# The inverse of the delta rule two units later, and the norm of its output on VectorE

## The chip, the cores and the metric

The kernel runs on one core of a Trainium2 chip. The metric is the device time of one execution, in microseconds (us); of several executions the median is taken. The core's engines are named as in the profile: PE (TensorE, the matmuls), PEld (its weight loads), DVE (VectorE), ACT (ScalarE), POOL (GpSimd) and SP, which here only issues DMAs. Each engine works through its own instructions in the order of the program, and waits on semaphores for the others.

## What is computed

Two blocks run one after the other on 256 positions of width 1024, all in float32. The first has a gated short convolution, a gated delta rule of 8 heads (its output is y_b), and a feed-forward part with a convolution; the second has dilated attention, retention and a feed-forward part. The change touches the delta rule. Its reference, cut to what matters (T is the 256 positions; the kernel uses two chunks of 128 where the reference has four of 64, which is the same function):

```
proj = rmsnorm(x) @ w_in;  bg, cg, xv, q, k, v, z, a, b, ga, gb = split(proj)
y_a = (bg * conv(cg * xv)) @ w_a_out
# delta rule, for each head and chunk:
L = strict_lower((k*beta) @ k.T) * decay
u, w = solve(I + L, [v*beta, k*beta*exp(G)])     # "the inverse"
o = chunked scan over (q, k, u, w)
o = o * rsqrt(mean(o*o) + EPS) * norm_g          # "the norm of its output"
y_b = (o * silu(z)) @ w_b_out
mix = sigmoid(ga) * y_a + sigmoid(gb) * y_b;  x = x + mix @ w_o
```

## The kernel before, in words

**Dense work in units.** Every weight matrix is cut into jobs of one block of 1 MB (128 partitions by 2048 floats), and nearly every job into two units of half a block. A unit is 24 matmuls of 256 columns (line 355): a weight half is split by ACT into a high part H (line 165) and by DVE into the rest L (line 168), and the three products high x high, high x low and low x high are summed. In the delta rule's neighbourhood the jobs come in this order: v's columns of w_in (4 jobs), w_a_out (4), then the columns of ga, z and gb (4 each), then w_b_out (4). The blocks come into three buffers "raw" by DMAs on SP's queue (line 337); the load of a job is issued when the last split of the job three before it is done. There are three buffers each for H and L, and a unit's split stands in the program two units ahead of its matmuls.

**The delta rule between the units.** The loop over units lets generators advance: after each unit's matmuls every open generator runs to its next `yield`, so a `yield` is the way to move work one unit later. The order of the instructions on every engine follows from where the yields stand. If a unit's input isn't there yet when its matmuls are to be written, `drain` advances the generators until it is, and what they write then stands ahead of the unit.

**The inverse.** `subst` inverts the 32x32 blocks of the triangular matrices by substitution, on DVE and then on POOL (tile ebd, with bt for the products). The result goes through DRAM: POOL writes ebd to a scratch tensor (scr), transposes it and writes it again, and eight DMAs (line 633, four on POOL's queue, four on SP's) bring the blocks to the tiles Em and Dm. `for _ in range(SC_Z): yield` then counts off units, and `sub_ok` lets `gdn_main` go on: line 688 multiplies Dm by U, lines 690, 691, 709 and 711 merge the blocks into the whole inverse, one batch per unit. Then follow the transposes of v (725), the products with the inverse (754), and those of o (766, 771, 743, 744).

**The norm and the way out.** The sums of squares of o are made by ACT (tile jk, into so). POOL scales them, DVE seeds the inverse root fo, POOL makes three Newton steps (helper `rsqrt`), and POOL multiplies o by fo, eight times. Four yields later PE transposes o in four pieces of two heads (line 808), one piece per unit; DVE multiplies a piece by g and zs, ACT writes its high part to Oh, and DVE the rest to Ol. Oh and Ol together are `ob`, the input of w_b_out's units. A unit of w_b_out uses half of the heads: the first half the pieces 0 and 1, the second half the pieces 2 and 3.

Of the kernel before, what the change touches and what calls it, by code (L numbers as in the profile page):

```python
# [8 lines left out]
I32 = mybir.dt.int32  # L9
# [3 lines left out]
MUL, ADD, SUB = ALU.mult, ALU.add, ALU.subtract  # L13

EPS = 1e-6
# [16 lines left out]
SG_Y = {8: 3, 0: 4, 16: 5}  # L32
U_Y = 1
SC_Y = 2
SC_Z = 6
EXP1 = 1


# [60 lines left out]
def _build(tc, nc, A, ACT, DVE, POOL, PE, SP, raw_p, hl_p, c_p, b_p, t_p, m_p, s_p, d_p, x_p):  # L99
    uid = [0]  # L100

    def nm(s):
        uid[0] += 1
        return f"{s}{uid[0]}"
# [33 lines left out]
    def free(*ts):  # L138
        for t in ts:
            tag, long = tag_of.pop(id(t))[0:2]  # L140
            free_tags[long].insert(0, tag)

    def tmp(tag, shape=(2, 256), dt=F32, bufs=None):
        return t_p.tile([128] + list(shape), dt, tag=tag, name=nm(tag), **({"bufs": bufs} if bufs else {}))

    def cst(name, shape, dt=F32):
        return c_p.tile(list(shape), dt, tag=name, name=name)
# [19 lines left out]
    def tt(eng, out, a, b, op):  # L167
        eng.tensor_tensor(out=out, in0=a, in1=b, op=op)  # L168

    def stt(out, in0, scalar, in1, op0, op1):  # L170
        DVE.scalar_tensor_tensor(out=out, in0=in0, scalar=scalar, in1=in1, op0=op0, op1=op1)

    def ts(out, in0, s1, op0, s2=None, op1=None):
        if s2 is None:
            DVE.tensor_scalar(out=out, in0=in0, scalar1=s1, scalar2=None, op0=op0)
        else:
            DVE.tensor_scalar(out=out, in0=in0, scalar1=s1, scalar2=s2, op0=op0, op1=op1)
# [8 lines left out]
    def pts(out, in0, s1, op0, s2=None, op1=None):  # L186
        if s2 is None:
            POOL.tensor_scalar(out=out, in0=in0, scalar1=s1, scalar2=None, op0=op0)
        else:
            POOL.tensor_scalar(out=out, in0=in0, scalar1=s1, scalar2=s2, op0=op0, op1=op1)  # L190

    def rsqrt(y, v, n, steps=3, dve=False):
        a = tmp(f"nw{n}", (n,))
        DVE.tensor_scalar(out=y.bitcast(I32), in0=v.bitcast(I32), scalar1=-0.5, scalar2=float(0x5F3759DF), op0=MUL, op1=ADD)
        for _ in range(steps):
            if dve:
                tt(DVE, a, y, y, MUL)
                stt(a, a, -0.5, v, MUL, MUL)
                stt(y, a, 1.5, y, ADD, MUL)
                continue  # L200
            tt(POOL, a, y, y, MUL)
            tt(POOL, a, a, v, MUL)
            pts(a, a, -0.5, MUL, 1.5, ADD)
            tt(POOL, y, y, a, MUL)
# [245 lines left out]
    def gates():  # L450
# [34 lines left out]
        yield  # L485
        yield from gdn_decay()
        yield from gdn_main()

    def gdn_norm_k():
# [84 lines left out]
    def gdn_main():  # L574
# [3 lines left out]
        srk, bk2, rqs = (gd[k] for k in ("srk", "bk2", "rqs"))  # L578
# [23 lines left out]
        def subst():  # L602
# [31 lines left out]
            free(ebd)  # L634
            for _ in range(SC_Z):
                yield
# [28 lines left out]
        a = tmp("nw16", (16,))  # L665
# [6 lines left out]
        rq2 = cst("ss2", [128, 2, 8]).rearrange("p c h -> p (c h)")  # L672
# [111 lines left out]
        sof = so.rearrange("p c h -> p (c h)")  # L784
        fo = cst("fo", [128, 16])
        yield
        tt(POOL, sof, sof, rq2, MUL)
        POOL.tensor_scalar(out=sof, in0=sof, scalar1=1.0 / 128, scalar2=EPS, op0=MUL, op1=ADD)
        yield
        rsqrt(fo, sof, 16)  # L790
        tt(POOL, fo, fo, rqs, MUL)
        for h2 in range(4):
            for c in range(2):
                sl = slice(8 * c + 2 * h2, 8 * c + 2 * h2 + 2)
# [896 lines left out]
```

## Time and profile before

| | us |
|---|---|
| median of 3 executions (1129.2 to 1130.95) | 1130.07 |
| the profiled execution | 1132.15 |
| its span in the trace | 1130.4 |
| PE busy in the span | 1107.6 |
| DVE busy | 755.6 |
| ACT busy | 584.9 |
| POOL busy | 242.9 |

PE is busy nearly all the time, so what counts is where it stands still and where its clock is low. In the page's forty slices the granted clock (1.0 is full speed, 2.4 GHz; 0.5 is 1.2 GHz) is below 0.9 in one slice alone, the seventh (170 to 198 us), which also has PE's lowest busy share. The views below look there, and then at the end of the delta rule.

### The profile page before, as it was taken

The page shows a single profiled execution, that of the slowest core. Times are in us where ns is not written, and L with a number is a line of the kernel's source. Part 1 is how long each engine was busy: PE and PEld are TensorE (multiplying, and loading weights), DVE is VectorE, ACT ScalarE, POOL GpSimd, SP SyncE. Part 2 cuts the span into 40 slices and gives each one's busy share as a digit, 9 for nine tenths or more (in the row PEclk, how much of TensorE's full clock was granted, in tenths as well). Part 3 has the DMA queues.
Part 4 walks back from the last instruction along what each step waited for, and adds up shares of the span by engine and source line. Part 5 has one row for each costly group of instructions (what it writes and reads, how often), then busy time and mean ns, then how long its engine had stood idle before and what let it go on. Part 6 is the DMA issues. An engine that isn't in the chain of part 4 may idle for free.

```text
span 1130.4 us, 20225 instructions
## 1 busy us (share of the span) xinstructions
PE 1107.6 (98%) x8340; PEld 1051.7 (93%) x8340; DVE 755.6 (67%) x1033; ACT 584.9 (52%) x944; POOL 242.9 (21%) x245
## 2 busy tenths in 40 slices
PE   9999897999999999999999999999999999999998
PEld 8989897999999999999878899889999999999997
DVE  4978995344577988778854567556686658655554
ACT  6866253266555444443687554445475445444442
POOL 2565796010401221222200500001340001000000
PEclk9999998999999999999999999999999999999999
DMA  8456347343555565554575544354447555565662
GB/s 262 128 186 186 118 149 197 102 150 112 187 187 169 169 210 193 193 183 162 185 260 182 186 150 150 126 189 133 150 143 227 189 186 166 180 197 190 194 192 75
DMA packets 155087, 194.82 MB, mean 172 GB/s; under 512 B 5678, under 2 KB 132005, under 8 KB 154740
## 3 DMA queue, kind: packets, MB, share of 16 engines
q1 hardware_dynamic: 153888, 191.57, 52.1%
q0 software_dynamic: 912, 1.43, 0.6%
q8 instruction: 65, 1.06, 0.4%
q10 hardware_dynamic: 196, 0.54, 0.1%
q14 instruction: 26, 0.21, 0.1%
HBM read 191.68 MB, written 1.84 MB: 171 GB/s over the span
## 4 chain that ended last, share of the span: by engine, by line
PE 82%; POOL 4%; DVE 2%; ACT 2%; issue 1%; DMA 1%; DVEq 0%; ACTq 0%; POOLq 0%
PE d L355 61%; PE x L355 13%; POOL ebd L168 2%; POOL bt L168 2%; DVE L L168 1%; ACT H L165 1%; DMA Dm<-scr 1%; ACT jk L165 1%; PE x L688 0%; PE x L1206 0%; PE x L1231 0%; PE x L690 0%; ACT w L165 0%; PE x L1265 0%; PE x L691 0%
## 5 line engine op out<-in xcount | busy, mean ns | idle before, releaser
L168 DVE TENSOR_TENSOR L<-raw,H 128x1024 fp32r<-128x1024 f32 x354 | 445.3, 1264 | 241.2 <-ACT H L165 240.9
L165 ACT ACTIVATE H<-raw 128x1024 fp32r<-128x1024 f32 (+1 forms) x355 | 369.4, 1053 | 188.8 <-PE d L355 122.3
L355 PE MATMUL d<-Hh,L 128*128 128x256 f32 x576 | 79.7, 281 | 8.0 <-DVE L L168 8.0
L355 PE MATMUL d<-nh,H 128*128 128x256 f32 x608 | 84.1, 280 | 0.0
L355 PE MATMUL d<-nl,H 128*128 128x256 f32 x608 | 84.1, 280 | 0.0
L355 PE MATMUL d<-nh,L 128*128 128x256 f32 x608 | 83.7, 279 | 0.0
L355 PE MATMUL d<-Hh,H 128*128 128x256 f32 x576 | 81.6, 284 | 0.7 <-ACT H L165 0.7
L355 PEld LDWEIGHTS d<-Hh,L 128*128 128x128 f32 x576 | 72.1, 188 | 10.1 <-DVE L L168 10.0
L355 PE MATMUL d<-Hl,H 128*128 128x256 f32 x576 | 79.1, 280 | 0.0
L355 PEld LDWEIGHTS d<-nh,H 128*128 128x128 f32 x608 | 77.6, 188 | 1.1
L355 PEld LDWEIGHTS d<-nl,H 128*128 128x128 f32 x608 | 76.8, 188 | 0.0
L355 PEld LDWEIGHTS d<-nh,L 128*128 128x128 f32 x608 | 76.7, 188 | 0.0
L355 PEld LDWEIGHTS d<-Hh,H 128*128 128x128 f32 x576 | 71.7, 188 | 1.1 <-ACT H L165 1.0
L355 PEld LDWEIGHTS d<-Hl,H 128*128 128x128 f32 x576 | 72.5, 188 | 0.0
L355 PE MATMUL d<-H,x2h 128*128 128x512 f32 x208 | 57.4, 398 | 0.8 <-ACT H L165 0.8
L355 PE MATMUL d<-H,x2l 128*128 128x512 f32 x208 | 57.0, 396 | 0.0
L355 PE MATMUL d<-L,x2h 128*128 128x512 f32 x208 | 56.4, 393 | 0.0
L355 PE MATMUL d<-x2h,H 128*128 128x256 f32 x384 | 54.2, 284 | 0.0
L355 PE MATMUL d<-x2l,H 128*128 128x256 f32 x384 | 52.7, 280 | 0.0
L355 PE MATMUL d<-x2h,L 128*128 128x256 f32 x384 | 52.3, 279 | 0.0
L165 ACT ACTIVATE w<-w 128x512 f32<-128x512 f32 (+1 forms) x35 | 21.7, 619 | 53.2 <-POOL w L168 22.0
L355 PEld LDWEIGHTS d<-x2h,H 128*128 128x128 f32 x384 | 48.5, 189 | 0.6
(403 smaller groups left out, 1943.7 us busy)
## 6 DMA issues: line engine op xcount, KB each, us to landing
raw<-in_w_in_dram SPq DMA_DIRECT2D x86, 1024.0 KB, 5.1
raw<-in_w_up_dram SPq DMA_DIRECT2D x38, 1024.0 KB, 5.3
raw<-in_w_down_dram SPq DMA_DIRECT2D x27, 1024.0 KB, 4.9
raw<-in_w_proj_b_dram SPq DMA_DIRECT2D x8, 1024.0 KB, 5.4
raw<-in_w_a_out_dram SPq DMA_DIRECT2D x4, 1024.0 KB, 9.1
raw<-in_w_b_out_dram SPq DMA_DIRECT2D x4, 1024.0 KB, 5.3
raw<-in_w_o_dram SPq DMA_DIRECT2D x4, 1024.0 KB, 5.9
raw<-in_w_out_dram SPq DMA_DIRECT2D x4, 1024.0 KB, 5.4
```

Of the source, the lines that this page charges most:

```text
L165: ACT.activation(out=out, in_=in_, func=func, **kw)
L168: eng.tensor_tensor(out=out, in0=a, in1=b, op=op)
L355: PE.matmul(out, lhsT=x if swap else w, rhs=w if swap else x, start=first and ps == 0, stop=last and ps == group[-1] and group is (order o ...
```

## The change

The constant SC_Z, the number of units between the DMAs into Em and Dm and the rest of the inverse, goes from 6 to 8. The norm of o is made on DVE alone: the scaling of so, the seed, the three Newton steps (three instructions each, where POOL had four) and the product with rqs. The seed and the first step stand behind the first `yield`, the other two steps behind the second. The products of o by fo stay on POOL.

```
-SC_Z = 6
+SC_Z = 8
...
         fo = cst("fo", [128, 16])
         yield
-        tt(POOL, sof, sof, rq2, MUL)
-        POOL.tensor_scalar(out=sof, in0=sof, scalar1=1.0 / 128, scalar2=EPS, op0=MUL, op1=ADD)
-        yield
-        rsqrt(fo, sof, 16)
-        tt(POOL, fo, fo, rqs, MUL)
+        tt(DVE, sof, sof, rq2, MUL)
+        ts(sof, sof, 1.0 / 128, MUL, EPS, ADD)
+        a = tmp("nw16", (16,))
+        DVE.tensor_scalar(out=fo.bitcast(I32), in0=sof.bitcast(I32), scalar1=-0.5, scalar2=float(0x5F3759DF), op0=MUL, op1=ADD)
+        for k in range(3):
+            tt(DVE, a, fo, fo, MUL)
+            stt(a, a, -0.5, sof, MUL, MUL)
+            stt(fo, a, 1.5, fo, ADD, MUL)
+            if k == 0:
+                yield
+        tt(DVE, fo, fo, rqs, MUL)
         for h2 in range(4):
...
```

On PE, where the inverse goes on, the order of before is this (Hh and Hl are the input's high and low part for v's columns; yah and yal are w_a_out's input; each group of three rows is a unit):

```order
L355 MATMUL d_2257<-Hh_114,H_2211 128x256 x8
L355 MATMUL d_2257<-Hl_115,H_2211 128x256 x8
L355 MATMUL d_2257<-Hh_114,L_2212 128x256 x8
L688 MATMUL x_2315<-Dm_1342,U_1114 128x64 x8
L355 MATMUL d_2338<-yah_1242,H_2249 128x256 x8
L355 MATMUL d_2338<-yal_1243,H_2249 128x256 x8
L355 MATMUL d_2338<-yah_1242,L_2250 128x256 x8
L688 MATMUL x_2365<-Dm_1342,U_1114 128x64 x8
L355 MATMUL d_2338<-yah_1242,H_2283 128x256 x8
```

and the order of the changed kernel at the same place is this:

```order
L355 MATMUL d_2257<-Hh_114,H_2211 128x256 x8
L355 MATMUL d_2257<-Hl_115,H_2211 128x256 x8
L355 MATMUL d_2257<-Hh_114,L_2212 128x256 x8
L355 MATMUL d_2329<-yah_1242,H_2249 128x256 x8
L355 MATMUL d_2329<-yal_1243,H_2249 128x256 x8
L355 MATMUL d_2329<-yah_1242,L_2250 128x256 x8
L355 MATMUL d_2329<-yah_1242,H_2283 128x256 x8
L355 MATMUL d_2329<-yal_1243,H_2283 128x256 x8
L355 MATMUL d_2329<-yah_1242,L_2284 128x256 x8
L688 MATMUL x_2387<-Dm_1342,U_1114 128x64 x8
L355 MATMUL d_2402<-yah_1242,H_2321 128x256 x8
```

The two batches of line 688 moved behind the two units of w_a_out's first job.

On PE, at the end of the delta rule, the order of before has a unit behind each of the transposes of o (the last two of the four stand here), and w_b_out's first unit (the one with Oh) after that:

```order
L808 MATMUL x_3589<-cmats,o_2834 128x128 x4
L355 MATMUL d_3599<-Hh_114,H_3517 128x256 x8
L355 MATMUL d_3599<-Hl_115,H_3517 128x256 x8
L355 MATMUL d_3599<-Hh_114,L_3518 128x256 x8
L808 MATMUL x_3628<-cmats,o_2834 128x128 x4
L355 MATMUL d_3599<-Hh_114,H_3555 128x256 x8
L355 MATMUL d_3599<-Hl_115,H_3555 128x256 x8
L355 MATMUL d_3599<-Hh_114,L_3556 128x256 x8
L355 MATMUL d_3672<-Oh_3509,H_3595 128x256 x8
```

and the changed kernel (where line 814 is the old line 808) has this:

```order
L814 MATMUL x_3607<-cmats,o_2896 128x128 x4
L355 MATMUL d_3578<-Hh_114,H_3536 128x256 x8
L355 MATMUL d_3578<-Hl_115,H_3536 128x256 x8
L355 MATMUL d_3578<-Hh_114,L_3537 128x256 x8
L814 MATMUL x_3646<-cmats,o_2896 128x128 x4
L814 MATMUL x_3661<-cmats,o_2896 128x128 x4
L355 MATMUL d_3656<-Oh_3566,H_3574 128x256 x8
L355 MATMUL d_3656<-Ol_3567,H_3574 128x256 x8
L355 MATMUL d_3656<-Oh_3566,L_3575 128x256 x8
L355 MATMUL d_3656<-Oh_3566,H_3613 128x256 x8
```

The dense units between the last transposes and w_b_out are gone, and the fourth transposes stand right behind the third.

On DVE, the pieces 2 and 3 of before (w is the product of a transposed piece, g and zs) stand with a weight's low part between them:

```order
L168 TENSOR_TENSOR L_3596<-raw_3422,H_3595 128x1024
L171 SCALAR_TENSOR_TENSOR w_3624<-x_3589,prm,zs_3132 128x512
L168 TENSOR_TENSOR Ol_3510<-w_3624,Oh_3509 128x512
L168 TENSOR_TENSOR L_3634<-raw_3422,H_3633 128x1024
L171 SCALAR_TENSOR_TENSOR w_3663<-x_3628,prm,zs_3132 128x512
L168 TENSOR_TENSOR Ol_3510<-w_3663,Oh_3509 128x512
```

and in the changed kernel they stand like this:

```order
L168 TENSOR_TENSOR L_3653<-raw_3480,H_3652 128x1024
L171 SCALAR_TENSOR_TENSOR w_3657<-x_3646,prm,zs_3101 128x512
L168 TENSOR_TENSOR Ol_3567<-w_3657,Oh_3566 128x512
L171 SCALAR_TENSOR_TENSOR w_3666<-x_3661,prm,zs_3101 128x512
L168 TENSOR_TENSOR Ol_3567<-w_3666,Oh_3566 128x512
L168 TENSOR_TENSOR L_3695<-raw_3480,H_3694 128x1024
```

The fourth piece now follows the third directly, and the next weight's low part comes behind both.

## Rows read from the trace of the kernel before

**Rows 1.** Page, part 1: engine, busy us (share of the span), instructions.
```profile
PE 1107.6 (98%) x8340; PEld 1051.7 (93%) x8340; DVE 755.6 (67%) x1033; ACT 584.9 (52%) x944; POOL 242.9 (21%) x245
```
**Rows 2.** Who waited for whom, PE, whole run: us in total, times, longest us.
```profile
PE d L355 <- DVE L L168: 8.0, 8, 2.5
PE x L688 <- DMA Dm<-scr: 6.6, 1, 6.6
```
**Rows 3.** Order of time: start, us, engine, line, operation, out<-in, count [idle before <-releaser].
```profile
174.61 1.09 PE L355 MATMUL d<-Hh,L 128*128 128x256 f32 x8
...
176.04 13.38 SPq L337 DMA_DIRECT2D raw<-in_w_a_out_dram  x4
...
182.34 3.65 PE L688 MATMUL x<-Dm,U 128*128 128x64 f32 x16 [6.65 <-DMA Dm<-scr]
184.02 2.00 ACT L165 ACTIVATE H<-raw 128x1024 fp32r<-128x1024 f32 x2 [3.80 <-DMA raw<-in_w_a_out_dram]
...
185.75 2.06 PE L355 MATMUL d<-yah,H 128*128 128x256 f32 x8
...
190.75 1.89 PE L688 MATMUL x<-Dm,U 128*128 128x64 f32 x16
...
192.45 1.19 PE L355 MATMUL d<-yah,H 128*128 128x256 f32 x8
```
**Rows 4.** Who waited for whom, SP's queue, 140 to 235 us.
```profile
SPq L633 <- DMA scr<-ebd: 16.0, 2, 13.9
```
**Rows 5.** Stretches: length, each engine's busy us (instructions), PEclk, DMA share, GB/s.
```profile
180.00:182.30 2.30, 0.00 (x0) 0.00 (x0) 0.00 (x0) 0.22 (x1) 0.52 (x1) 0.53 1.08 328
...
189.00:190.00 1.00, 1.00 (x7) 1.00 (x6) 1.00 (x2) 0.45 (x1) 1.00 (x1) 0.50 0.02 5
190.00:191.00 1.00, 1.00 (x9) 1.00 (x9) 1.00 (x1) 1.00 (x2) 1.00 (x2) 0.80 0.69 179
...
206.80:208.00 1.20, 1.20 (x10) 1.18 (x9) 1.07 (x3) 0.00 (x0) 0.00 (x0) 0.78 1.08 384
208.00:210.00 2.00, 2.00 (x11) 2.00 (x11) 0.00 (x1) 0.00 (x0) 0.00 (x0) 0.50 0.31 108
210.00:211.00 1.00, 1.00 (x7) 1.00 (x7) 0.00 (x0) 0.00 (x0) 0.00 (x0) 0.56 0.00 0
```
**Rows 6.** Order of time again, at the third and fourth transposes of o.
```profile
305.03 0.60 PE L808 MATMUL x<-cmats,o 128*128 128x128 f32 x4
...
305.39 1.17 PE L355 MATMUL d<-Hh,H 128*128 128x256 f32 x8
...
306.07 0.63 ACT L165 ACTIVATE Oh<-w 128x512 fp32r<-128x512 f32 x1 [1.96 <-DVE w L171]
...
306.73 0.69 DVE L168 TENSOR_TENSOR Ol<-w,Oh 128x512 fp32r<-128x512 f32 x1 [0.70 <-ACT Oh L165]
...
308.17 1.23 DVE L168 TENSOR_TENSOR L<-raw,H 128x1024 fp32r<-128x1024 f32 x1 [0.74 <-ACT H L165]
308.26 0.60 PE L808 MATMUL x<-cmats,o 128*128 128x128 f32 x4
...
309.31 0.74 DVE L171 SCALAR_TENSOR_TENSOR w<-x,prm,zs 128x512 f32<-128x512 f32 x1
...
310.09 0.63 ACT L165 ACTIVATE Oh<-w 128x512 fp32r<-128x512 f32 x1 [1.95 <-DVE w L171]
...
310.75 0.69 DVE L168 TENSOR_TENSOR Ol<-w,Oh 128x512 fp32r<-128x512 f32 x1 [0.70 <-ACT Oh L165]
```
**Rows 7.** Groups by line on DVE, 128 to 142 us and 360 to 368: busy us, mean ns.
```profile
L168 DVE TENSOR_TENSOR nw<-grr 128x16 f32<-128x16 f32 x3 | 1.7, 569 | 0.0
...
L168 DVE TENSOR_TENSOR nw<-sr 128x2 f32<-128x2 f32 x3 | 0.5, 161 | 0.1
```
**Rows 8.** Order of time, behind the norm: a low part and PE's use of it.
```profile
288.39 1.22 DVE L168 TENSOR_TENSOR L<-raw,H 128x1024 fp32r<-128x1024 f32 x1
...
292.13 1.09 PE L355 MATMUL d<-Hh,L 128*128 128x256 f32 x8
```

## The prediction

> **What bounds the kernel now.** The page's first part has TensorE (PE) busy for 98% of the span [rows 1]; PE runs the matmuls in the order of the program, so a matmul that waits holds up all behind it. The second view is who waited for whom: the longest single wait of the run is 6.6 us, PE at line 688 (first matmuls of the inverse) for the DMA into Dm; next come eight waits for DVE's low parts, 8.0 us together, 2.5 us the longest [rows 2]. The third view is the instructions in order of time around that wait [rows 3]: PE ends the last unit of V at 175.7, stands until 182.34, runs line 688, and starts the first unit of w_a_out at 185.75.
>
> The reader should now ask what stands behind the removed wait. The block of w_a_out was issued on SP's queue at 176.04, and ACT's split of it into H waited for that DMA until 184.02 [rows 3]. The queue was held up itself: SP waited 16.0 us at line 633 for the scratch results of the substitution, 13.9 us at a stretch [rows 4]. So two transfers end late here, the blocks of Dm at 182.34 and the weights at 184.02, and only the first shows as a wait of PE, because line 688 stood ahead of the weights' matmuls.
>
> **Term 1, the inverse two units later.** In the new order two units of w_a_out stand where line 688 stood. SP's rows up to this point are unchanged, and nothing that the substitution does is moved, so I let the weights land when they do now. The first unit needs the first H only: one of the two splits that begin at 184.02 and take 2.00 us together [rows 3], so 1.00, done at 185.02; with 0.1 us to hand over, PE restarts at 185.1 instead of 182.34. The wait doesn't go, it grows from 6.6 to 9.4 us, and line 688's 3.4 us (182.34 to 185.75), which lay inside the wait for the weights, now stand between units that have work. All the work that PE now does from 182.34 on is done from 185.1 on: **+2.8 us**. After that I find nothing that absorbs it: the same view of PE's waits, asked for 192 to 316, lists none.
>
> The clock gives part of this back. It is at 0.53 in 180 to 182.3, at 0.50 until 190 and at 0.80 in the us after, so it rises at about 190.4; that is 8.1 us after PE restarted, but 4.65 us after its first full-size matmul at 185.75 [rows 3, 5]. At half clock, 8.1 us cost 4.0 us. With the change the full-size matmuls come first. If the clock again rises 4.65 us behind the first of them, the slow stretch is 4.65 us and costs 2.3, a gain of **1.7 us**; line 688 then runs in the 1.7 us that its second half takes at full clock (190.75 to 192.45). The ends are no gain (again 8.1 us) and 2.3 us of gain (3.4 us, the length of the other slow stretch, from about 207.5 to 210.9, worked out from the means of 206.8 to 208 and 210 to 211 [rows 5]). Term 1 is **+1.1 us**, between +0.5 and +2.8.
>
> **Term 2, the far end of the chain.** All that the delta rule does later moves two units back too, up to the transposes of o (line 808) and the split into Oh and Ol, which feeds w_b_out. Now a dense unit stands behind each of the four transposes. In the new order the third and the fourth stand back to back, and w_b_out's first unit right behind them. Its first unit needs heads 0 to 3 (pieces 0 and 1 of Oh), its second heads 4 to 7 (pieces 2 and 3).
>
> I lay the new order on the old times, with the third transposes at 305.03 [rows 6], where piece 1 of Oh is being made. Both transposes end their issue by 305.7 (0.36 each, 305.03 to 305.39). A unit of 24 matmuls takes 2.87 us (305.39 to 308.26), four matmuls 0.48. On DVE and ACT the order of one piece stays as it is: low part of a weight, product with zs, Oh on ACT, Ol. Piece 1 of Oh ends at 306.70, piece 2 at 310.72, its Ol at 311.44 [rows 6]. Piece 3 comes directly behind: product 0.74 (312.2), Oh 0.63 (312.9), with the hand-overs as in piece 2.
> - Unit 1: four matmuls from 305.7 to 306.2, then a wait for piece 1 until 306.8: 0.6 us.
> - Unit 2 could start at 309.1 and waits for piece 2 until 310.75: 1.65 us.
> - Four matmuls later (311.2) it waits for piece 3 until 312.9: 1.7 us.
>
> Together **+3.9 us**, all on PE's path, since PE has no other work before these units. Below, I bound it by 1.0 (only the first wait and some hand-over, if DVE and ACT run ahead of their present pace), above by the 3.9 and the clock. For the gaps may lower the clock: it fell at about 207.5 although PE was busy throughout the small matmuls of the inverse [rows 5], so it needs no standstill. One slow stretch of 3.4 us costs 1.7 us; I take half, **+0.85**, with 0 and 1.7 as ends. The Trainium skill's page "TensorE: Matmul & The Clock Gate", section "HAM oscillation — how this bites in real kernels", lays the fall to long idle gaps between bursts of matmuls; by that alone these short gaps leave the clock up and the sum is 1135.1, while [rows 5] show a fall with no gap at all, and by that the sum is 1136.8.
>
> **Term 3, the norm on VectorE.** POOL loses 15 small instructions (so twice, four for each of three steps, fo by rqs), and DVE gains 12 (so twice, three for each step, fo by rqs). With the seed, which was on DVE already, 13 stand there, six ahead of one low part L and seven ahead of the next. What they cost is bounded by two rows of the same chain: 0.57 us a piece in the norm of q, with POOL busy in the substitution, and 0.16 us on 128x2, with POOL idle [rows 7]. The POOL rows between are empty in the new order, so I take 0.17: 6 x 0.17 = 1.0 us ahead of the first L. That L has slack: it starts at 288.39, ends at 289.6, and PE uses it at 292.13 [rows 8], 2.5 us later. Seven more, 1.2 us, meet an L with a unit more of slack. So **0**; if the cover went, the first six would cost 3.4 - 2.5 = 0.9 us at 0.57 each. Nothing is gained either: no wait of PE for POOL, or for o, stands in [rows 2], so fo that is ready earlier releases nobody; the products o by fo stay on POOL. DVE now waits itself for the sums of squares on ACT, but a weight's H stands behind them on ACT and its L ahead of the norm on DVE, so that wait is over when DVE gets there. The Trainium skill's page "SBUF — State Buffer", section "Who interferes with whom", has one port pair that VectorE and GpSimd share as an exclusive lock; [rows 7] agree, 0.57 against 0.16, and by it the norm would cost 13 x 0.57 = 7.4 us of DVE only with POOL at work beside it.
>
> **Sum.** 1.1 + 3.9 + 0.85 + 0 = 5.85, so 5.9 us. The profiled execution took 1132.15 us (span 1130.4), 2.1 us more than the median of 1130.07; a profiled run of the changed kernel would take about 1138.0, the median **1136.0**. What this kernel's times tell from no change is about 0.2%, 2.3 us, so "slower" begins at 1132.3.
>
> **Rivals.**
> *The wait for Dm really goes (faster, 1125).* If the weights of w_a_out were in SBUF by 175.7, PE would go on through two units to 181.4, wait 0.9 us for Dm and keep its clock: 6.6 - 0.9 = 5.7 and 4.0 us gained, against 4.75 of term 2, so 1130.1 - 4.95 = 1125.1. For it speaks that the waits name Dm alone [rows 2]; against it ACT's wait for the DMA until 184.02 and SP's 16.0 us [rows 3, 4], which the change doesn't touch. It decides in its favour from a landing about 6 us earlier. 0.08.
> *Term 2 is small (same, 1132).* If the last pieces come at PE's pace, so that only about 1 us is waited: 1130.1 + 1.1 + 1.0 = 1132.2. For it: DVE has idle time there. Against: the four steps of a piece stand in a chain across two engines behind a weight's split, and it is 4.0 us from one Oh to the next (306.07 to 310.09) where PE takes 3.2 from one of the transposes to the next (305.03 to 308.26) [rows 6]. 0.16.
> *The norm holds back the low parts (slower, 1138.5).* The longest wait for an L now is 2.5 us [rows 2]; one more such behind the 12 new instructions gives 1136.0 + 2.5. Against: the slack of [rows 8] and a free POOL. 0.08.
> *The forecast*, 1132.5 to 1139: 0.68.
>
> **How the numbers follow.** Slower: 0.68 + 0.08 = 0.76; same 0.16; faster 0.08. The bounds give 0.5 + 1.0 = 1.5 below (1131.6) and 2.8 + 3.9 + 1.7 + 0.9 = 9.3 above (1139.4). The range from 1131 to 1140 leaves out the first rival and the outer parts of the others, under 2 in 10.
>
> **What would show it.** In PE's waits, line 688 for Dm is gone, and a wait of about 9.4 us stands at w_a_out's first unit, put down to ACT's H; the H behind it waits for the DMA of w_a_out until about 184. Line 688 runs later without a wait. At w_b_out's first two units stand waits for Oh of 0.6, 1.65 and 1.7 us. DVE has nw at about 0.17 us, POOL has none of it there, and no new wait for an L stands behind them. The prediction is wrong if the weights land well before 184, if the waits at Oh are missing, or if PE goes on from 175.7.

## The result, and the profile after

The changed kernel took 1137.03 us (median of 6 executions, 1136.04 to 1137.49) against 1130.49 for the kernel before beside it: ratio 1.0057, interval 1.0044 to 1.0070, so 5 to 8 us slower. The prediction was 1136.0. The profiled execution took 1136.79 us, its span 1135.0; that of before 1132.15 and 1130.4.

The first part of the page of the changed kernel (engine, busy us, share of the span, instructions) answers to [rows 1]:

```profile
PE 1110.9 (98%) x8340; PEld 1054.5 (93%) x8340; DVE 758.2 (67%) x1045; ACT 585.5 (52%) x944; POOL 238.9 (21%) x230
```

POOL lost 15 instructions and DVE gained 12, as the diff says. PE has the same 8340 and is busy 3.3 us longer. Most of that is the clock: of PE's busy time 6.0 us are lost to a granted clock below 1.00 in before's trace and 8.6 in this one (each stretch's busy time by the missing part of its clock). 3.3 of the 8.6 are lost at 139 to 147 us, ahead of everything that the change moved. The other 1.3 us of the longer span are time in which PE stood. Who waited for whom on PE, whole run (us in total, times, longest us), answers to [rows 2]:

```profile
PE d L355 <- DVE L L168: 7.9, 7, 2.6
PE d L355 <- ACT H L165: 7.0, 3, 5.6
PE d L355 <- ACT Oh L165: 2.9, 3, 1.4
```

The wait of line 688 for Dm (6.6 us) is gone. Two new ones stand in its place: 5.6 us for a high part H, and 2.9 us for Oh. The order of time at the first of them, all engines (start, us, engine, line, operation, out<-in, count [idle before <-releaser]), answers to [rows 3]:

```profile
175.07 12.39 SPq L337 DMA_DIRECT2D raw<-in_w_a_out_dram  x4
...
176.50 1.09 PE L355 MATMUL d<-Hh,L 128*128 128x256 f32 x8
...
177.20 0.63 ACT L165 ACTIVATE w<-w 128x512 f32<-128x512 f32 x1 [7.11 <-POOL w L168]
...
182.06 2.00 ACT L165 ACTIVATE H<-raw 128x1024 fp32r<-128x1024 f32 x2 [2.78 <-DMA raw<-in_w_a_out_dram]
...
183.17 2.08 PE L355 MATMUL d<-yah,H 128*128 128x256 f32 x8 [5.58 <-ACT H L165]
...
190.85 1.89 PE L688 MATMUL x<-Dm,U 128*128 128x64 f32 x16
```

PE ends V's last unit at 177.6 and stands until 183.17, because ACT can split w_a_out's weights only when they land at 182.06, and SP issued them only at 175.07. Line 688 comes later, without a wait. V's last unit itself ends 1.9 us later than in before (175.7); the slow stretch at 139 to 147, which before's trace doesn't have, is the likely reason. The order of time on PE at the second place, the end of the delta rule, answers to [rows 6]:

```profile
309.64 1.03 PE L814 MATMUL x<-cmats,o 128*128 128x128 f32 x8
310.43 0.72 PE L355 MATMUL d<-Oh,H 128*128 128x256 f32 x4
311.31 0.74 PE L355 MATMUL d<-Oh,H 128*128 128x256 f32 x4 [0.17 <-ACT Oh L165]
...
315.33 0.74 PE L355 MATMUL d<-Oh,H 128*128 128x256 f32 x4 [1.40 <-ACT Oh L165]
317.38 1.22 PE L355 MATMUL d<-Oh,H 128*128 128x256 f32 x4 [1.31 <-ACT Oh L165]
318.40 1.91 PE L355 MATMUL d<-Ol,H 128*128 128x256 f32 x8
...
321.27 1.10 PE L355 MATMUL d<-Oh,H 128*128 128x256 f32 x8
```

The third and fourth transposes of o stand in one batch of eight, w_b_out's units right behind them. The first unit starts at 310.43, 1.05 us earlier than in the profiled execution of before; the third starts at 321.27, 4.27 us later than there:

```profile
311.48 1.07 PE L355 MATMUL d<-Oh,H 128*128 128x256 f32 x8
...
317.00 1.07 PE L355 MATMUL d<-Oh,H 128*128 128x256 f32 x8
```

So in this pair of executions all of the loss, 5.3 us, lies in these eleven microseconds. Eight matmuls take 1.91 us instead of 1.1 there, which is the clock. It is in the view by stretches, PE alone (length, PE's busy us and instructions, granted clock, DMA share, GB/s), which answers to [rows 5]:

```profile
181.00:184.00 3.00, 0.83 (x4) 0.50 1.10 350
184.00:187.00 3.00, 3.00 (x16) 0.50 0.98 309
187.00:188.00 1.00, 1.00 (x8) 0.77 0.05 17
...
206.00:208.00 2.00, 2.00 (x12) 0.51 0.00 0
...
318.00:320.00 2.00, 2.00 (x11) 0.50 0.00 0
```

### The profile page after: what moved, and what is told of

Read it like the earlier page. It is cut to its first block, busy times and chain, and to the rows that moved or that the text cites. A ratio compares the mean times of both kernels' runs of the same rounds, so it can differ in the third digit from the quotient of the medians.

```text
span 1135.0 us, 20221 instructions
## 1 busy us (share of the span) xinstructions
PE 1110.9 (98%) x8340; PEld 1054.5 (93%) x8340; DVE 758.2 (67%) x1045; ACT 585.5 (52%) x944; POOL 238.9 (21%) x230
## 4 chain that ended last, share of the span: by engine, by line
PE 84%; POOL 5%; DVE 4%; ACT 3%; DMA 3%; issue 2%; SPq 0%; DVEq 0%; ACTq 0%; POOLq 0%
PE d L355 62%; PE x L355 13%; POOL bt L168 2%; POOL ebd L168 2%; DVE L L168 1%; ACT H L165 1%; PE d L292 1%; DVE w L171 1%; DMA raw<-in_w_a_out_dram 1%; DMA raw<-in_w_in_dram 1%; ACT jk L165 1%; PE x L1212 0%; PE x L1237 0%; DMA gam<-gs 0%; ACT w L165 0%
## 5 line engine op out<-in xcount | busy, mean ns | idle before, releaser
L355 PEld LDWEIGHTS d<-x2l,H 128*128 128x128 f32 x384 | 48.3, 188 | 0.0
```

What stands on the lines that cost most here:

```text
L355: PE.matmul(out, lhsT=x if swap else w, rhs=w if swap else x, start=first and ps == 0, stop=last and ps == group[-1] and group is (order o ...
```

## The experiments

Theory: the moved inverse costs it all, by two things, the wait for w_a_out's weights (term 1) and the end (term 2); the norm costs nothing. Rivals: the norm costs part of it; or whatever is put later loses the same in another form.

### One half of the change at a time

The inverse alone (the kernel before):

```
-SC_Z = 6
+SC_Z = 8
```

> SC_Z = 8 alone, the norm stays on POOL. Theory (the moved inverse costs all of it, most at w_b_out's first units): 1136 to 1138, as the whole change; PE waits for Oh of about 3 us. Rival (the norm on DVE costs it): about 1130.5, as before.

Measured: 1137.59 us, ratio to before 1.0057 (1.0044 to 1.0069), the same as the whole change. PE's waits in it:

```profile
PE d L355 <- ACT H L165: 9.7, 3, 8.2
...
PE d L355 <- ACT Oh L165: 2.7, 2, 1.4
```

The norm alone (the changed kernel with `SC_Z = 6`):

> The norm on DVE alone, SC_Z = 6. Theory: 1130.5 within 1 us, the small instructions take 0.17 us each and PE waits for no low part behind them. Rival (the norm costs it): 1135 or more, with waits of PE for L of 2.5 us or more after 285 us.

Measured: 1131.19 us, ratio 1.0003 (0.9994 to 1.0012). The wait for Dm is back:

```profile
PE x L688 <- DMA Dm<-scr: 5.2, 1, 5.2
```

So the norm has no part in the time that shows (the interval leaves it at most 1.4 us), and the moved inverse has all of it.

### The end: two tries

First the transposes of o two units sooner, by two yields fewer:

```
         yield
         yield
-        yield
-        yield
         Oh, Ol = alloc_hi("Oh"), ...
```

> The whole change, but two of the four yields ahead of the transposes of o are taken away, so the transposes stand again ahead of four dense units. Theory: the waits for Oh go and the clock stays up there, about 5 us back: 1131.5 to 1133, less about 1 us if the first transposes now wait for the products o by fo on POOL. Rival (the longer wait at the inverse costs it): 1136 to 1137 as the whole change, since nothing is altered there.

Measured: 1136.31 us, ratio 1.0049 (1.0035 to 1.0063). The time expected was missed. The waits for Oh did go, but PE now came to the transposes before POOL had made the products o by fo. PE in order of time there:

```profile
299.31 0.33 PE L812 MATMUL x<-cmats,o 128*128 128x128 f32 x1 [0.61 <-POOL o L168]
300.86 0.55 PE L812 MATMUL x<-cmats,o 128*128 128x128 f32 x3 [1.22 <-POOL o L168]
301.16 1.90 PE L355 MATMUL d<-Hh,H 128*128 128x256 f32 x8
```

1.8 us of waits, and the clock at half behind them. That is the rival's picture, but by a cause of this edit: it took the two units from the products. The second try takes one unit from the products and the other from the pause in the middle of the norm:

```
-            if k == 0:
-                yield
...
-        yield
         yield
         yield
         yield
         Oh, Ol = alloc_hi("Oh"), ...
```

> The changed kernel with only its end altered: the norm's Newton steps in one go (no unit between the first and the second) and three units instead of four before the transposes of o, so that the transposes stand two units sooner, where they stand in the kernel before, while the products o*fo keep three units to finish. My theory: what the later inverse costs is paid at the end, by the third and fourth transposes of o lying back to back so that the first units of w_b_out wait 0.17, 1.40 and 1.31 us for Oh, and by the clock fall behind these waits (3.4 us slow, 1.7 lost). Then both go and 4 to 5 of the 5.9 us return: 1131.5 to 1133.5, waits for Oh under 0.3 us, no wait for o in front of the transposes, clock 1.00 from 310 to 325. Rival: whatever is put later loses the same in another form, as the wait for o did with two units sooner (1136.3): then 1135.5 to 1137, with a wait of 1 us or more at the transposes or a clock fall there.

Measured: 1133.16 us, ratio 1.0021 (1.0012 to 1.0030). No wait for Oh is left; 0.7 us for o is, which wasn't expected. Its waits of PE, whole run:

```profile
PE d L355 <- ACT H L165: 8.4, 3, 7.0
...
PE x L811 <- POOL o L168: 0.7, 1, 0.7
```

So the end costs 1137.03 - 1133.16 = 3.9 us, or 6.5 - 2.1 = 4.4 us if each kernel is taken against the kernel before beside it. What is left against before (1131.04 beside it) is 2.1 us, with a wait for H of 7.0 us, longer than the changed kernel's 5.6.

### The stop in front of w_a_out: three layers

The weights issued ahead of the transfers of Em and Dm (the changed kernel, the number of units in front of and behind these):

```
-SC_Y = 2
-SC_Z = 8
+SC_Y = 4
+SC_Z = 6
```

> The DMAs into Em and Dm stand two units later in the program (SC_Y 4, SC_Z 6, so the inverse goes on at the same unit as in the whole change), which puts the first block of w_a_out ahead of them on SP's queue; the norm on DVE, four yields at the end. Theory: the first weights land well before 175, PE goes through two units of w_a_out without the wait of 5.6 to 9.4 us and line 688 waits under 2 us; the clock stays up; waits for Oh stay. 1137 - 8 = 1128 to 1131. Rival (PE's wait there is Dm's transfer, not the weights): no gain, 1136 to 1137.

Measured: 1134.19 us, ratio 1.0025 (1.0016 to 1.0034): 2.8 us better than the changed kernel, where 6 or more were expected. SP and ACT in order of time:

```profile
161.60 0.37 SPq L337 DMA_DIRECT2D raw<-in_w_a_out_dram  x1
```
```profile
177.16 0.63 ACT L165 ACTIVATE w<-w 128x512 f32<-128x512 f32 x1 [8.80 <-POOL w L168]
177.70 1.55 ACT L165 ACTIVATE w<-d,prm 128x256 f32<-128x256 f32 x4
179.13 2.02 ACT L165 ACTIVATE H<-raw 128x1024 fp32r<-128x1024 f32 x2
```

The weights were issued 13.5 us sooner, and still H starts only at 179.13. It stands on ACT behind a sigmoid of V's convolution that waited 8.80 us for POOL. POOL in order of time there:

```profile
168.33 2.31 POOL L624 COPY ebd<-ebd 64x1024 f32<-64x1024 f32 x1
...
171.47 1.83 POOL L627 MEMSET P<- 128x2048 f32 x1
173.22 1.34 POOL L633 DMA_DIRECT2D Em<-scr  x2
174.56 1.29 POOL L633 DMA_DIRECT2D Dm<-scr  x2
175.86 2.48 POOL L168 TENSOR_TENSOR w<-w,w 128x510 f32<-128x510 f32 x2
```

POOL's addition for V (175.86) stands behind the tail of the substitution: the last steps, a copy, a memset and the issue of four DMAs, one after the other with gaps of at most 0.3 us. The expectations further down speak of a wait of GpSimd for the scratch transfers; the trace shows none (0.3 us ahead of each of POOL's two writes to scr, and that for POOL's own work), POOL is simply busy. The same sigmoid waited 7.11 us in the changed kernel too, only there the weights came later still.

The two repairs together, and then also V's addition taken off POOL:

```
-            tt(POOL, acc[:, :, 1:256], acc[:, :, 1:256], a2[:, :, 0:255], ADD)
+            tt(DVE if base == 16 else POOL, acc[:, :, 1:256], acc[:, :, 1:256], a2[:, :, 0:255], ADD)
```

> As e7_end_units, and the first block of w_a_out issued on SP ahead of the transfers of Em and Dm as in e4_weights_ahead (4 units before, 6 behind them). My theory (two separate costs that add): e4_weights_ahead gave 1134.2 with 2.9 us of waits for Oh left; without these and their clock fall 1129.5 to 1131. The wait at the first unit of w_a_out stays near 4.4 us, for H behind ACT's sigmoid that waits for POOL. Rival: the two edits work on the same loss, and the time stays at 1131.5 to 1134.

Measured: 1130.62 us, ratio 0.9995 (0.9986 to 1.0004). From the changed kernel that is 6.4 us, where the two edits alone gave 2.8 and 3.9: they add up within about 1 us. The wait for H is 5.5 us at its longest, where 4.4 were expected.

> As e8_ahead_end, and the convolution's last addition for the four V blocks on VectorE instead of GpSimd, so that ACT's sigmoid no longer stands behind GpSimd's wait for the scratch transfers. My theory: the stop of PE in front of w_a_out has three layers, Dm, then w_a_out's block on SP, then ACT held by GpSimd; with all three gone PE doesn't stop there and the clock doesn't fall (4.4 us of wait and some 2 of clock): 1124 to 1127. Rival a: a fourth layer comes in its place, Dm late again because its transfers are issued behind the weights: L688 waits 2 to 5 us and the time is 1128 to 1131. Rival b: VectorE's addition, in order with L, holds back L by 0.6 us in each of four units: 1127 to 1129 with waits for L.

Measured: 1124.24 us, ratio 0.9941 (0.9929 to 0.9954), faster than either kernel. PE's waits, whole run, and the stretch in question:

```profile
PE d L355 <- DVE L L168: 8.0, 8, 2.7
...
PE d L355 <- ACT H L165: 1.4, 2, 0.8
```
```profile
180.00:188.00 8.00, 7.67 (x66) 1.00 0.79 250
```

PE stands for 0.3 us in all there, and the clock stays up. Neither rival came: no wait for Dm, and the waits for L are what they were.

That addition alone, with weights and end as in the changed kernel:

> The changed kernel with one edit: the convolution's last addition for the four V blocks on VectorE instead of GpSimd. w_a_out's first block stays behind the transfers of Em and Dm on SP. Theory of layers (the stop of PE in front of w_a_out ends when the last of SP's block and ACT's sigmoid is through, and in the changed kernel that is SP's block, at 182.06): the stop stays, 1135.5 to 1138, H waits for raw, 5 us or more at PE. Rival: ACT's hold behind GpSimd was the real cause and the early weights only a part of it: then 1131 to 1133, and the stop falls under 2 us.

Measured: 1136.26 us, ratio 1.0060 (1.0047 to 1.0074): nothing gained that is clear of the noise. ACT and PE there:

```profile
183.15 2.00 ACT L165 ACTIVATE H<-raw 128x1024 fp32r<-128x1024 f32 x2 [11.62 <-DMA raw<-in_w_a_out_dram]
```
```profile
184.25 2.08 PE L355 MATMUL d<-yah,H 128*128 128x256 f32 x8 [8.80 <-ACT H L165]
```

With ACT free, ACT itself waits 11.62 us for the weights. So the last layer by time is the weights, under it ACT behind POOL; each hides the other.

Is the later inverse worth anything, then? The inverse back in the place that it has in the kernel before, with the weights ahead and V's addition on DVE:

```
-SC_Y = 2
-SC_Z = 8
+SC_Y = 4
+SC_Z = 4
```

> The inverse in the place that it has in the kernel before (4 units in front of the transfers of Em and Dm, 4 behind), the first block of w_a_out ahead of them on SP, the V addition on VectorE, norm and end as in the changed kernel. My theory: the stop in front of w_a_out goes as in e9_ahead_end_vadd, but L688 stands two units nearer and may wait for Dm: the transfers on GpSimd and SP are issued at 173 to 176 us and land some 4 us behind, L688 comes near 180: wait 0 to 3 us, time 1125 to 1130. If the later place had bought something of its own, this kernel is slower than e9_ahead_end_vadd by 2 us or more; if not, the same within 1 us.

Measured: 1131.41 us, ratio 1.0003 (0.9994 to 1.0011), with PE's wait

```profile
PE x L688 <- DMA Dm<-scr: 7.1, 1, 7.1
```

where I had expected 0 to 3, so the time was missed as well. POOL issued the last transfer into Dm at 176.4, and the slowest of the four took 6.1 us from issue to landing, where I had put 4; in before's trace the slowest took 6.1 us too. So the early weights and the free ACT buy nothing while line 688 stands in front. Against the fastest kernel the difference is 1131.41 - 1124.24 = 7.2 us, but that kernel has the end repaired too, which the later place needs and the place of before doesn't (no wait for Oh here). Against the next kernel, which has the same norm and yields as this one, the two units later are worth 1131.41 - 1129.01 = 2.4 us (1.9 if each is taken against the kernel before beside it). So the later place pays only with the front repaired, and most of it only with the end repaired as well.

Last, the front repaired and the end left as the change has it:

> e9_ahead_end_vadd with the end of the changed kernel left as it is (norm in two parts, four units before the transposes): weights ahead on SP and the V addition on VectorE alone. If the end costs by itself what e7_end_units gave back (1137.0 to 1133.2), whatever stands in front: 1124.2 + 3.9, 1127.5 to 1129, with about 2.9 us of waits for Oh. Rival: with the stop in front of w_a_out gone the work arrives earlier against the weights and the end costs more or less than that: 1125 to 1126.5, or over 1130.

Measured: 1129.01 us, ratio 0.9983 (0.9973 to 0.9994), 4.8 us above the kernel with the end repaired and at the top of what was expected. The end costs by itself, whatever stands in front, a little more than the 3.9 us above.

## Why the prediction was right, point by point

**The forecast** was a sum of 5.9 us over before; 6.5 us were measured (1137.03 - 1130.49). Its two large terms can be told apart by the kernel with the end repaired: 2.1 us for the front and 4.4 for the end, where 1.1 and 4.75 were said. The path was right at both ends. That the sum came within 0.6 us is in part luck: inside both terms the sizes are further off than that, and cancel.

**Term 1, the weights (+1.1, between +0.5 and +2.8): right in kind, rough in size.** The wait didn't go, it moved to w_a_out's first unit, on ACT's H behind the DMA. But 9.4 us were said and 5.6 stand in the trace (8.2 with the inverse alone, 7.0 with the end repaired). The step that failed is "I let the weights land when they do now". H started at 184.02 in the profiled execution of before [rows 3], and at 182.06, 181.81, 182.17, 182.65 and 183.15 in the five with the later inverse and the weights' issue as it was (the changed kernel, the inverse alone, the end repaired, the end two units sooner, the addition alone), but also at 182.69 in the kernel with the norm alone, which has the order of before: I took one execution's landing for the kernel's. The prediction named weights that land "well before 184" as a sign of being wrong; H started 2.0 us sooner than there, and 1.0 of it is that SP issued the weights sooner. PE restarted at 183.17, and not at 185.1. That is half of the 3.8 us by which the wait was mis-sized; the other half is PE itself, which ended V's last unit 1.9 us later than in before. The clock step held in kind: with full-size matmuls first the slow stretch lasted from PE's restart at 183.17 to about 187.5, 4.3 us where 4.65 were said. That it came so near is luck: in the six other traces where w_a_out's units stand first behind the stop it lasted 3.1 to 6.0 us, and 7.6 to 8.1 in the three (before among them) where line 688 does. With the earlier restart the front costs nothing in the profiled pair (w_b_out's first unit stands 1.05 us earlier than in before), while the medians of the kernel with the end repaired and of before say +2.1 (by the interval 1.4 to 3.4). The profiled execution of before (1132.15) lies above all 27 later ones beside the end repair, and that of the end repair is the lowest of its 11 (1132.71). How much of the difference this makes, and how much the end repair's own 0.7 us of wait for o, stays open.

What the prediction didn't see is that the weights were not the only thing behind the wait. Its first rival ("the wait for Dm really goes", 1125) was to decide in its favour if the weights landed some 6 us earlier. With weights issued 13.5 us earlier that wasn't enough (1134.19), because ACT stood behind POOL. The row for it was in the trace of before as well (ACT, order of time):

```profile
178.13 0.63 ACT L165 ACTIVATE w<-w 128x512 f32<-128x512 f32 x1 [9.94 <-POOL w L168]
178.66 1.55 ACT L165 ACTIVATE w<-d,prm 128x256 f32<-128x256 f32 x4
```

So H couldn't have started ahead of 180.2 there, whenever the weights landed. But the view of PE's waits names only the releaser that came last, and SP's wait of 16.0 us [rows 4] explained the rest so well that I didn't ask what else stands on ACT's queue ahead of H. With both out of the way the rival's picture came true, no stop and a clock at 1.00, but not its size: 1129.01 with the end unrepaired, where it said 1125.1. With the end repaired it is 1124.24.

**Term 2, the end (+3.9 of waits, +0.85 of clock): right in its path and its total.** The waits for Oh are 0.17, 1.40 and 1.31 us, 2.9 in all, where 0.6, 1.65 and 1.7 were said; what was mis-sized is the pace of the pieces (Oh begins at 307.10, 310.63, 314.65 and 316.70 in the changed kernel: 3.5 us from the first to the second, where [rows 6] have 4.0, and 2.05 from the third to the fourth, where 2.2 were said). The clock fell behind these waits in the profiled execution, from about 317 to 321, which costs some 1.4 us (PE's busy time from 316 to 322 by the missing part of the clock); half of such a fall, 0.85, was in the sum. Whether it comes is open in each execution: of the five traces with these waits two show no fall there. What the end costs without a clock fall stands in the last kernel's trace, where the clock stays at 1.00 behind the same waits:

```profile
299.61 0.72 PE L355 MATMUL d<-Oh,H 128*128 128x256 f32 x4
...
309.02 1.07 PE L355 MATMUL d<-Oh,H 128*128 128x256 f32 x8
```

From w_b_out's first unit to its third it is 9.4 us there (and in the kernel with the addition alone), 10.8 in the changed kernel and 5.5 in before: 3.9 us without the fall, and 1.4 for the fall. So the 3.9 of the sum came out as a total, though the waits are only 2.9 of it. Most of the other 1.0 is a term that the sum didn't have: Oh's matmuls now come in groups of four that take 0.72 to 0.74 us each, where eight in one go take 1.07. That the two misses cancel is luck. Repaired, the end gave back 3.9 to 4.4 us, against 4.75 said.

**Term 3, the norm (0): right.** DVE in order of time, first and last of the 13 and the low part between them:

```profile
293.04 0.17 DVE L168 TENSOR_TENSOR so<-so,ss 128x16 f32<-128x16 f32 x1
...
294.18 1.22 DVE L168 TENSOR_TENSOR L<-raw,H 128x1024 fp32r<-128x1024 f32 x1
...
296.56 0.18 DVE L168 TENSOR_TENSOR fo<-fo,rqs 128x16 f32<-128x16 f32 x1
```

0.17 us a piece, as the nearer row of [rows 7] had it (POOL is busy for only 0.1 us from 292 to 297); no new wait for L; and the kernel with the norm alone doesn't differ from before. It is worth something only afterwards: made in one go, on DVE, it gave the end one of the two units that the repair needed.

**The rivals.** "Term 2 is small" fell (2.9 us of waits and 3.9 us in all, not 1.0); "the norm holds back the low parts" fell (1131.19).

## What to carry to other kernels

A wait removed from the engine that sets the time shows the next thing that was late at the same place; before moving work, follow every engine and queue that feeds the next instructions (here SP's, ACT's and, behind ACT, POOL's) to the time at which each would have let go on its own. An edit can be right and still lose: two units later cost 6 us alone, and were worth 2 us once the weights went ahead and one addition left the busy POOL, and 7 us once the end was repaired as well. And a chain that is moved later has an end; ask who uses its last piece, and whether there is still other work to put in between.

## What was not expected of the hardware

**The clock falls in some executions and not in others, at the same work.** The kernel with the front repaired and the end not has the same waits for Oh (2.9 us) as the changed kernel, and here are its stretches (length, PE's busy us, instructions, granted clock, DMA share, GB/s) around 140, 200 and 316 us, the three places where others fell:

```profile
138.00:146.00 8.00, 6.36 (x50) 1.00 0.42 133
...
196.00:212.00 16.00, 16.00 (x135) 1.00 0.23 73
310.00:322.00 12.00, 12.00 (x106) 1.00 0.67 217
```

Its waits for Oh lie at 300 to 307, and the clock is at 1.00 there too. This execution took 1124.46 us, the least of 12 of this kernel, whose highest is 1130.55. The fastest kernel's profiled execution, by its median the better by 4.8 us, took 1125.14, with two falls:

```profile
138.00:146.00 8.00, 6.08 (x28) 0.58 0.42 131
...
196.00:202.00 6.00, 6.00 (x38) 0.72 0.00 0
```

So one profiled execution of each would have put these two kernels the other way round. Of the twelve profiled kernels, before included, ten show a fall between 196 and 214 us, during or after the small matmuls of the inverse with PE busy all the time, five one at 138 to 147, and three of the five that wait 2.7 to 2.9 us for Oh a fall behind these waits. The other executions have no trace, but each has its mean granted clock on record. In the 12 of the kernel with the front repaired it goes from 0.999 in the fastest (1124.46) over 0.997 (1127.11) to 0.993 in the slowest (1130.55); 0.006 of 1124 us is 6.7 us, and their spread is 6.1. So in this kernel the spread goes with the clock and has its size; where in the program it fell isn't on record. Four of the fastest kernel's five have 0.998, and the profiled one, its slowest, 0.995. The slower executions have the lower clock in the kernels with the addition alone and with the early weights too; in the others no clear order shows.

The Trainium skill's page "TensorE: Matmul & The Clock Gate", section "HAM oscillation — how this bites in real kernels", lays such falls to idle gaps between bursts. For the stop in front of w_a_out the traces agree: in all ten that have it (4.4 to 8.8 us) the clock is at 0.50 afterwards, and in the two without it (PE stands 1.1 us at most) at 1.00. The falls between 196 and 214 us, with no gap in the trace, don't fit it.

**A queue that waits holds back everything behind it.** SP's wait for the scratch results held up weights that had no part in them: issue at 175.07, against 161.60 when put ahead. The Trainium skill's page "DMA: Bandwidth & Descriptors" says, in its section "Anatomy of one DMA — SWDGE (gpsimd) path", that DMA engines don't wait on semaphores and the issuing sequencer does so before dispatch; the section is about DMAs that GpSimd issues, and here, where SP issued them, the two issue times agree with it.
